# Layer 0's conditioning products in steps of four weight pieces, and two places instead of three for the split weights beside them

## The chip, the cores and the metric

The kernel runs on one core of one Trainium2 chip. The time is in device microseconds (us), from the start to the end of one execution. Engines: TensorE (PE; PEld are its weight loads), VectorE (DVE), ScalarE (ACT), GpSimd (POOL), and SyncE (SP), which here only asks for transfers (DMA).

## The reference, cut to what matters

Two layers, one of stick-breaking attention and one of gated linear attention, over 512 prompt tokens and 8 sequences of 16 sample tokens (T = 640 tokens in all, width 2048). Each layer first makes `shift, scale, gate` from a conditioning vector of each of the 9 sequences:

```python
shift, scale, gate = jnp.split(c @ w_ada[i] + b_ada[i], 3, axis=-1)   # c: 9 x 2048, w_ada[i]: 2048 x 6144
h = rmsnorm(x, norm_g[i]) * (1 + scale[:, None]) + shift[:, None]
q, k, v, zg = jnp.split(h @ w_in, 4, axis=-1)                         # layer 0: w_in 2048 x 8192
x = x + gate[:, None] * y
```

## The kernel before, in words

Big products in fp32 run as three passes on rounded halves: `halves` (L134, L135) makes of each piece a rounded part `wh` by a cast on ACT and the rest `wl` by a subtraction on DVE, and a product is `wh*hi + wh*lo + wl*hi`. A piece of weights is 128 x 1024 fp32, 512 KB.

Layer 0's input product is done mainly by `by_sevens`: the 2048 x 256 block of weights of a job (28 jobs, one for each 256 columns of q, k, v and z that earlier code leaves over) is cut in four quarters b11, b12, b21, b22, and seven products of eighths replace eight (a Strassen scheme). A job's seven products, called P1 to P7 here, are 24 matmuls each (L583, 128 x 320). Their weights are, in order: b11; b11 + t3, where t3 = b22 - b12 (L546, L550); b21; t3; b12 - b11 (L547); b21 less the second (L555); b22. The splits of these seven are called w1 to w7 here. `weights()` makes them ahead, DVE and ACT in an order that the build's scheduler sets, TensorE in the written order.

Places: raw pieces lie in four places `wb` and two `wr`. The next job's four loads are asked for by `fetch` in the course of a job; each starts when its place comes free, and the next job's b22 comes last: it takes the place that b12 leaves when w5 has been made. Split weights lie in rings: two places of `wh` and `wl` in the pool `wp`, and a third in `ring3["pool"]`, which every third call of `split` uses:

```python
third = ring3["pool"] is not None and n % 3 == 0
h, lo = ((ring3["pool"] if third else wp).tile([P, 1024], F32R, tag=t, name=t[:2], bufs=1 if third else 2)
         for t in (ring3["tags"] if third else ("wh", "wl")))
```

A split can begin when the product that last used its place has ended. With three places w(n) waits for the product three back, with two for the product two back, that is, for the start of the product just ahead.

Beside the sevens runs the side lane `rest_of_ada`: both halves of layer 0's gate, layer 1's shift and scale (four calls of `ada_mod`, L180) and a half of layer 1's gate (`ada_gate`, L222). One *step* loads `group` pieces `ar`, waits for its turn (`tiled=True`), and then multiplies each of them by the conditioning columns `cT`, 32 wide, as four 32 x 256 matmuls on four column strips of the array. `Side.tick` runs a tiled step only if `side.every` us have passed since the last by the lane's own count of TensorE's time. A step's loads are asked for as the step before frees their places.

Of the kernel before, what the change touches and what calls it, by code (L numbers as in the profile page):

```python
# [8 lines left out]
F32 = mybir.dt.float32  # L9
# [6 lines left out]
P = 128  # L16
# [25 lines left out]
def hybrid_step_kernel(ctx: ExitStack, tc: tile.TileContext, A: dict, O: list):  # L42
# [11 lines left out]
    def by(l, r):  # L54

        n = r.free_size()
        if l.dtype == F32R:
            pe["now"] += n / 2400 + 0.0133
        elif l.free_size() <= 32:
            pe["now"] += n / pe["quad"] + 0.01  # L60
        else:
            pe["now"] += n / 600 + 0.005
        return r

    def block(x):

        pe["now"] += 0.11
        return x

    def load(out, in_):  # L70
        nc.sync.dma_start(out=out, in_=in_)
# [17 lines left out]
    ad = l0.enter_context(tc.tile_pool(name="ad", bufs=1, reuse_waits="tile"))  # L89
# [9 lines left out]
    def bank(tag):  # L99
        return psum["pool"].tile([P, 512], F32, tag=tag, name=f"ps_{tag}", bufs=psum["bufs"][tag])  # L100
# [36 lines left out]
    ring3 = {"n": 0, "pool": None, "tags": ("wh", "wl")}  # L137
# [23 lines left out]
    def ada_mod(pool, ring, i, j0, ns, tag, group, pace=None, close=None):  # L161


        w, each = P * ns, 2 // ns
        src = A["w_ada"][i].rearrange("(p kt) (q m) -> p kt q m", kt=KT, q=3)
        acc = None
        for kt in range(0, KT, each * group):
            rs = []
            for k in range(kt, kt + each * group, each):
                r = ring()  # L170
                for e in range(each):
                    load(r[:, 4 * w * e:4 * w * e + 4 * w].rearrange("p (q m) -> p q m", q=2),
                         src[:, k + e, 0:2, 256 * j0:256 * j0 + 2 * w])
                rs.append(r.rearrange("p (e q c) -> p e q c", e=each, q=4))
            yield step(pace(group) if pace else 0.5, tiled=True)
            if acc is None:
                acc = bank(tag)
            for m in range(each * group):
                for q in range(4):
                    mm(acc[32 * q:32 * q + 32, :w], cT[:, kt + m, :], by(cT[:, kt + m, :], rs[m // each][:, m % each, q, :]),  # L180
                       start=kt + m == 0, stop=kt + m == KT - 1)
        if close:
            close()
        row = pool.tile([P, 256], F32, tag="ada_r", name="ada_r")[:, :w]
        dve.tensor_copy(row, acc[:, :w])
        yield step(1.5, tp=1)
        tp = bank("tp")
        for s in range(ns):
            turn_block(tp[:, P * s:P * s + P], block(row[:, P * s:P * s + P]), ident)
        v = tp[:, :P * ns].rearrange("p (s t h r) -> p t h s r", s=ns, t=2, h=2)  # L190
        for h in range(2):
            ks = slice(2 * j0 + ns * h, 2 * j0 + ns * h + ns)

            def col(c0):
                return cols[:, c0 + ks.start:c0 + ks.stop].unsqueeze(2).to_broadcast([P, ns, NSEQ])

            sh, sc, b0 = sh_t[i][:, ks, :], sc_t[i][:, ks, :], 56 + 32 * i
            dve.tensor_tensor(sh, v[:, 0, h, :, :NSEQ], col(b0), op=ALU.add)
            dve.scalar_tensor_tensor(sc, v[:, 1, h, :, :NSEQ], 1.0, col(b0 + KT), op0=ALU.add, op1=ALU.add)
            dve.tensor_tensor(sc, sc, col(16 * i), op=ALU.mult)  # L200

    def ada_gate(pool, ring, i, tag, group, cT, halves_=(0, 1)):

        src = A["w_ada"][i].rearrange("(p kt) n -> p kt n", kt=KT)
        for hf in halves_:
            bias = pool.tile([P, 256], F32, tag="ada_bg", name="ada_bg")
            acc = None
            for j in range(4):
                n0 = 2 * D + 1024 * hf + 256 * j
                load(bias[32 * j:32 * j + 32, :], A["b_ada"][i, n0:n0 + 256].partition_broadcast(32))  # L210
            for kt in range(0, KT, group):
                rs = []
                for k in range(kt, kt + group):
                    r = ring()
                    load(r, src[:, k, 2 * D + 1024 * hf:2 * D + 1024 * hf + 1024])
                    rs.append(r)
                yield step(0.5, tiled=True)
                if acc is None:
                    acc = bank(tag)
                for m, r in enumerate(rs):  # L220
                    for j in range(4):
                        mm(acc[32 * j:32 * j + 32, :256], cT[:, kt + m, :], by(cT[:, kt + m, :], r[:, 256 * j:256 * j + 256]),  # L222
                           start=kt + m == 0, stop=kt + m == KT - 1)
            dve.tensor_tensor(bias, acc[:, :256], bias, op=ALU.add)
            for j in range(4):
                store(gate_d[i][:, 1024 * hf + 256 * j:1024 * hf + 256 * j + 256], bias[32 * j:32 * j + NSEQ, :])
# [47 lines left out]
    def step(wait=0.0, tp=0, z=0, tiled=False):  # L274
        return wait, tp, z, tiled
# [68 lines left out]
    side = Side()  # L344
# [390 lines left out]
    cT = ad.tile([P, KT, 32], F32, name="cT")  # L735
    nc.gpsimd.memset(cT, 0.0)

    def ad_ring():
        return ad.tile([P, 1024], F32, tag="ar", name="ar", bufs=2)
# [3 lines left out]
    with tc.tile_pool(name="st", bufs=1, reuse_waits="tile") as st:  # L743
# [46 lines left out]
        def pace(n):  # L790
            come["n"] += n
            return max(0.0, 18.0 + 1.4 * come["n"] - pe["now"])

        def ring(tags):
            n = 0
            while True:
                tag = tags[n % len(tags)]
                yield ad_ring() if tag is None else sp.tile([P, 1024], F32, tag=tag, name="ar")
                n += 1
# [32 lines left out]
        pe["quad"] = 2400  # L832


    def rest_of_ada():
        yield step(22.0)
        yield from ada_gate(ad, ad_ring, 0, "z", 2, cT)
        for k0 in range(0, 8, 2):
            yield from ada_mod(ad, ad_ring, 1, k0, 2, "z", 2)
        yield from ada_gate(ad, ad_ring, 1, "z", 2, cT, (0,))  # L840

    with tc.tile_pool(name="wq", bufs=1, reuse_waits="tile") as wq:
        def rows0(out, p, scratch, prompt, sample):

            cs = slice(256 * p, 256 * p + 256)

            def leave(g, n, tp):
                kr = slot(12 + g % 2, (P, 2, 256), F32, "kr")
                dve.tensor_copy(kr[:, :n, :], tp)
                if scratch is not None:  # L850
                    store(scratch[256 * g:256 * g + P * n, :].rearrange("(a p) n -> p a n", p=P), kr[:, :n, :])
                if g < 2:
                    store(prompt[256 * g:256 * g + 256, cs].rearrange("(a p) n -> p a n", p=P), kr)
                else:
                    store(sample[:, cs], kr[:, 0, :])

            return as_rows(out, leave)

        def keep_key(p):
            def f(out):  # L860
                keep_in(k_d[p])(out)
                side.add(rows0(out, p, None, kp_rows, ks_rows))
            return f

        def keep_value(p):
            return lambda out: side.add(rows0(out, p, v_d[p], vp_rows, vs_rows))

        jobs = []
        for p in range(NPAIR):
            jobs += [(D + 256 * p, keep_key(p)), (256 * p, keep_in(q_d[p]))]  # L870
            if p >= 2:
                jobs.append((2 * D + 256 * p, keep_value(p)))
        jobs += [(3 * D + 256 * p, keep_in(z_d[p])) for p in range(PLAIN, NPAIR)]
        side.every = 8.0
        side.add(rest_of_ada())
        ring3["pool"] = wq
        ring3["n"] = 0
        sevens = by_sevens(h1, w_in0, wq, jobs, given)
        for _ in range(2):
            next(sevens)  # L880
        for i in range(5):
            v01 = slot(8 + i, (P, 512), F32, "v01")
            (dve.tensor_copy if i % 2 else nc.scalar.copy)(v01, acc[i])
            for p in range(2):
                move(v_d[p][P * i:P * i + P, :], v01[:, 256 * p:256 * p + 256])
            move(vp_rows[P * i:P * i + P, 0:512] if i < 4 else vs_rows[:, 0:512], v01)
        ends.close()
        drive(sevens)
        side.finish()
        h1.again(0, wq)  # L890
        ring3["pool"] = None
# [308 lines left out]
    with tc.tile_pool(name="o0", bufs=1, reuse_waits="tile") as po, ExitStack() as only_d:  # L1200
# [136 lines left out]
        wq = only_d.enter_context(tc.tile_pool(name="wq1", bufs=1, reuse_waits="tile"))  # L1337
# [90 lines left out]
        n = 0  # L1428
# [469 lines left out]
    with tc.tile_pool(name="o1", bufs=1, reuse_waits="tile") as po:  # L1898
# [3 lines left out]
        for kt in range(10, 16):  # L1902
            r = po.tile([P, T], F32, tag="rows", name="og_in", bufs=6)
            load(r, og_d[kt // 4][:, kt % 4, :])
            n = 20 + 2 * kt % 12
# [44 lines left out]
        for c in range(3):  # L1950
            drive(hs_gemm512(og1, w_out1, 512 * c, lambda a, pt: add(a, c, pt), lambda: fetch_x1(c), piece=piece,
                             k0=8, nk=8))
# [41 lines left out]
```

## Time and profile before

| | |
|---|---|
| time, median of 3 runs | 2571.93 us (2571.87 to 2578.37) |
| profiled execution | 2568.07 us, its span 2566.3 us, mean granted clock 0.979 |
| busy in the span | PE 2442.6 us (95%), PEld 84%, DVE 63%, ACT 40%, POOL 6% |
| the sevens of layer 0 | about 153.6 to 937.8 us of the span |
| steps of `rest_of_ada` | 56, from 184.6 to 739 us |

A row of the timeline gives start, duration, engine, line, operation, out<-in, shape, how many of the same were merged, and in brackets the engine's idle time before it and what ended it. Matmuls overlap: the time that one costs is the distance between starts, not its duration. A row of windows gives a stretch, its length, the busy time of each engine with its instructions, the granted TensorE clock (1.00 is 2.4 GHz, 0.50 is 1.2 GHz), the busy share of the 16 DMA engines, and GB/s. Waits are engine, line, what was waited for: us in total, times, longest.

### The profile page before, as it was taken

How to read it: one execution, taken by the hardware profiler on the slowest of the kernel's cores; microseconds unless marked ns; L12 is line 12 of the kernel's file. 1: busy time of each engine (PE TensorE's matmuls, PEld its weight loads, DVE VectorE, ACT ScalarE, POOL GpSimd, SP SyncE). 2: the span in 40 equal slices, each digit the busy share in tenths (PEclk: the TensorE clock that was granted, in tenths of full speed). 3: DMA queues.
4: the chain of work that ended last, by engine and by line, in shares of the span. 5: the costliest groups of instructions: out<-in, count | busy, mean ns of one | idle time of the engine just before them, and what ended most of it. 6: DMA issues, size and time to landing. Idle time of an engine off the chain costs nothing.

```text
span 2566.3 us, 43469 instructions
## 1 busy us (share of the span) xinstructions
PE 2442.6 (95%) x17321; PEld 2146.9 (84%) x17321; DVE 1612.7 (63%) x2493; ACT 1018.4 (40%) x1796; POOL 165.0 (6%) x385
## 2 busy tenths in 40 slices
PE   6899999999999999999999989999999998889998
PEld 5589999998999998787777767999999997766776
DVE  5565555555666656666776677666666655656566
ACT  4332222222223335565444344333333364655133
POOL 0010000000000000000000000000000014334200
PEclk8899999999999999999999999999999999999999
DMA  9966666766654366766665863344444377777464
GB/s 347 317 192 217 226 207 198 242 217 197 219 186 123 118 210 212 232 214 212 224 215 175 241 203 122 99 113 129 121 127 120 112 223 254 243 237 233 170 233 146
DMA packets 452796, 502.04 MB, mean 196 GB/s; under 512 B 26090, under 2 KB 349810, under 8 KB 452466
## 3 DMA queue, kind: packets, MB, share of 16 engines
q1 hardware_dynamic: 430210, 436.86, 53.5%
q0 software_dynamic: 16048, 51.92, 6.0%
q10 hardware_dynamic: 6336, 10.49, 1.1%
q8 instruction: 136, 2.23, 0.4%
q14 instruction: 66, 0.54, 0.1%
HBM read 410.05 MB, written 89.13 MB: 195 GB/s over the span
## 4 chain that ended last, share of the span: by engine, by line
PE 76%; DVE 8%; DMA 7%; issue 4%; ACT 3%; POOL 1%; SPq 0%; ACTq 0%; POOLq 0%; DVEq 0%
PE ps_mm L583 40%; PE ps_mm L687 10%; PE ps_mm L641 4%; PE ps_mm L507 3%; PE ps_mm L367 3%; DMA gv<-kr 2%; PE ps_tp L1061 2%; PE ps_z L180 2%; PE ps_tp L1029 1%; PE ps_z L1005 1%; DVE wl L135 1%; PE ps_tp L1106 1%; PE ps_mm L1965 1%; PE ps_z L1074 1%; ACT wh L134 1%
## 5 line engine op out<-in xcount | busy, mean ns | idle before, releaser
L583 PE MATMUL ps_mm<-sums,wh 128*128 128x320 f32 x2880 | 646.0, 312 | 5.7 <-ACT wh L134 5.7
L583 PEld LDWEIGHTS ps_mm<-sums,wh 128*128 128x128 f32 x2880 | 483.3, 189 | 14.9 <-ACT wh L134 7.1
L583 PE MATMUL ps_mm<-h,wh 128*128 128x320 f32 x2160 | 483.2, 312 | 3.8 <-DVE u L589 3.8
L583 PE MATMUL ps_mm<-sums,wl 128*128 128x320 f32 x1440 | 447.6, 311 | 1.1 <-DVE wl L135 1.1
L583 PEld LDWEIGHTS ps_mm<-h,wh 128*128 128x128 f32 x2160 | 359.1, 188 | 20.0 <-issue 14.9
L135 DVE TENSOR_TENSOR wl<-wr,wh 128x1024 fp32r<-128x1024 f32 x190 | 232.3, 1224 | 215.7 <-ACT wh L134 214.3
L134 ACT CAST wh<-wb 128x1024 fp32r<-128x1024 f32 x178 | 186.8, 1049 | 444.7 <-PE ps_mm L583 379.0
L583 PE MATMUL ps_mm<-h,wl 128*128 128x320 f32 x1080 | 333.8, 309 | 0.2 <-DVE wl L135 0.2
L134 ACT CAST wh<-wr 128x1024 fp32r<-128x1024 f32 x190 | 199.4, 1050 | 320.0 <-PE ps_mm L583 196.2
L583 PEld LDWEIGHTS ps_mm<-sums,wl 128*128 128x128 f32 x1440 | 272.4, 189 | 1.8 <-DVE wl L135 1.8
L135 DVE TENSOR_TENSOR wl<-wb,wh 128x1024 fp32r<-128x1024 f32 x178 | 217.6, 1222 | 64.1 <-ACT wh L134 63.8
L687 PE MATMUL ps_mm<-wh,ogh 128*128 128x512 f32 x460 | 201.4, 438 | 14.2 <-ACT ogh L134 10.3
L641 PE MATMUL ps_mm<-h,wh 128*128 128x320 f32 x896 | 207.2, 318 | 7.9 <-ACT wh L134 5.2
L583 PEld LDWEIGHTS ps_mm<-h,wl 128*128 128x128 f32 x1080 | 202.8, 188 | 0.5 <-DVE wl L135 0.5
L687 PE MATMUL ps_mm<-wh,ogl 128*128 128x512 f32 x460 | 182.5, 397 | 0.4 <-DVE ogl L135 0.4
L687 PE MATMUL ps_mm<-wl,ogh 128*128 128x512 f32 x460 | 181.8, 395 | 0.0
L641 PEld LDWEIGHTS ps_mm<-h,wh 128*128 128x128 f32 x896 | 150.6, 190 | 19.3 <-issue 7.0
L641 PE MATMUL ps_mm<-h,wl 128*128 128x320 f32 x448 | 139.6, 312 | 1.4 <-DVE wl L135 1.4
L687 PEld LDWEIGHTS ps_mm<-wh,ogh 128*128 128x128 f32 x460 | 87.7, 191 | 44.6 <-issue 16.8
L943 DVE TENSOR_TENSOR_SCAN k<-k,zero_c 128x544 f32<-128x544 f32 (+4 forms) x96 | 93.2, 975 | 29.5 <-ACT k L939 16.6
L687 PEld LDWEIGHTS ps_mm<-wh,ogl 128*128 128x128 f32 x460 | 87.1, 189 | 21.7 <-DVE ogl L135 1.8
L687 PEld LDWEIGHTS ps_mm<-wl,ogh 128*128 128x128 f32 x460 | 87.9, 191 | 10.6
(352 smaller groups left out, 3785.2 us busy)
## 6 DMA issues: line engine op xcount, KB each, us to landing
ar<-in_w_ada_dram SPq DMA_DIRECT2D x160, 512.0 KB
wb<-in_sb_w_in_dram SPq DMA_DIRECT2D x82, 512.0 KB
kc<-in_cache_sb_k_dram SPq DMA_DIRECT2D x64, 512.0 KB
vc<-in_cache_sb_v_dram SPq DMA_DIRECT2D x64, 512.0 KB
wb<-in_gla_w_in_dram SPq DMA_DIRECT2D x51, 512.0 KB
wr<-in_gla_w_in_dram SPq DMA_DIRECT2D x45, 512.0 KB
wr<-in_sb_w_in_dram SPq DMA_DIRECT2D x44, 512.0 KB
ar<-in_w_ada_dram SPq DMA_DIRECT2D x64, 256.0 KB
```

The costliest lines, as they stand in the source:

```text
L134: nc.scalar.copy(hi, x)
L135: (e or dve).tensor_tensor(lo, x, hi.bitcast(F32), op=ALU.subtract)
L180: mm(acc[32 * q:32 * q + 32, :w], cT[:, kt + m, :], by(cT[:, kt + m, :], rs[m // each][:, m % each, q, :]), start=kt + m == 0, stop=kt + m ...
L367: mm(acc[a], l[:, c], by(l[:, c], r[:, k2, :]), start=kt == k0 and first, stop=kt == k0 + nk - 1 and last)
L507: mm(acc[a], l, by(l, r[:, e, :]), start=j == 0 and e == 0 and begun, stop=j == 7 and e == 1 and last)
L583: mm(acc, l[:, k, :], by(l[:, k, :], r), start=start and k == 0 and first, stop=k == 7 and last, skip_group_check=True)
L641: mm(acc[nt], l[:, k, :], by(l[:, k, :], r), start=k0 == 8 and k == 0 and first, stop=k0 == 0 and k == 7 and last)
L687: mm(acc, l, by(l, r[:, e, :]), start=i == 0 and e == 0 and first, stop=i == 1 and e == 1 and last)
L943: dve.tensor_tensor_scan(kr, kr, zeros[:, :w], 1.0, ALU.mult, ALU.add)
L1005: mm(z[:, :n], q[:, hh, qs], by(q[:, hh, qs], k[:, hh, :n]), start=True, stop=True)
L1029: mm(o[:, :P], l, by(l, aT[:, kb, :]), start=kb == 0, stop=kb == qb)
L1061: turn_block(tp[:, P * c:P * c + P], block(kc[:, c, P * hh:P * hh + P]), ident)
```

## The change

A step of the conditioning products takes four pieces instead of two (`group` 4), and a turn comes every 18 us of the lane's count instead of 8. The four `ar` places are the two of the pool `ad` and two in `wq`. The third place for split weights in `wq` goes, so that this stage splits into two places (later stages keep their third). Nothing of the arithmetic changes.

```diff
-    def rest_of_ada():
-        yield step(22.0)
-        yield from ada_gate(ad, ad_ring, 0, "z", 2, cT)
-        for k0 in range(0, 8, 2):
-            yield from ada_mod(ad, ad_ring, 1, k0, 2, "z", 2)
-        yield from ada_gate(ad, ad_ring, 1, "z", 2, cT, (0,))
...
-        side.every = 8.0
+        turn = [0]
+
+        def four():
+
+            turn[0] += 1
+            return ad_ring() if turn[0] % 4 < 2 else wq.tile([P, 1024], F32, tag="ar", name="ar", bufs=2)
+
+        def rest_of_ada():
+            yield step(22.0)
+            yield from ada_gate(ad, four, 0, "z", 4, cT)
+            for k0 in range(0, 8, 2):
+                yield from ada_mod(ad, four, 1, k0, 2, "z", 4)
+            yield from ada_gate(ad, four, 1, "z", 4, cT, (0,))
+
+        side.every = 18.0
         side.add(rest_of_ada())
-        ring3["pool"] = wq
-        ring3["n"] = 0
```

On TensorE the 56 steps of 8 matmuls become 28 of 16. Counted from job 0, they stand after half of P3 in jobs 5, 8, 11, 14, 17 and 20 and after P3 in job 2; after half of P5 in jobs 1, 4, 7, 10, 13, 16 and 19; the other 14 after P1 or P6 or in P7. Layer 0's later stages and layer 1 keep TensorE's order.

DVE in job 8, from the split w5 to w7. `wl_4003` and `wl_3983` are w5, the next split is w6, then t3 of the next job out of its b22 and b12, `u` is P4's sum and `out` P5's. Before:

```order
L135 TENSOR_TENSOR wl_4003<-wb_3621,wh_4002 128x1024
L135 TENSOR_TENSOR wl_4032<-wr_3625,wh_4031 128x1024
L546 TENSOR_TENSOR t3_4106<-wb_3909,wb_3907 128x1024
L589 TENSOR_TENSOR u_3898<-ps_mm_3946,m1_3897 128x320
L547 TENSOR_TENSOR wb_3907<-wb_3907,wb_3905 128x1024
L135 TENSOR_TENSOR wl_4062<-wb_3623,wh_4061 128x1024
```

Of the change:

```order
L135 TENSOR_TENSOR wl_3983<-wb_3625,wh_3982 128x1024
L589 TENSOR_TENSOR u_3890<-ps_mm_3938,m1_3889 128x320
L135 TENSOR_TENSOR wl_4036<-wr_3629,wh_4035 128x1024
L546 TENSOR_TENSOR t3_4098<-wb_3901,wb_3899 128x1024
L589 TENSOR_TENSOR out_3888<-ps_mm_4064,u_3890 128x320
L135 TENSOR_TENSOR wl_4066<-wb_3627,wh_4065 128x1024
L547 TENSOR_TENSOR wb_3899<-wb_3899,wb_3897 128x1024
```

The splits stand one product later: w6 now follows P4's sum, and t3 stands between w6 and w7, with P5's sum where P4's was. In the seven jobs with a step in or after P3, w7 follows t3 with only a sum near it (L547 behind w7); in the others L547 stands between t3 and w7.

SP at the same place of job 8; `wb_3907` and `wb_3899` are the next job's b12, the `wr` its b21, `wb_3909` and `wb_3901` its b22. Before:

```order
L71 DMA wb_3907<-in_sb_w_in_dram 128x8x128
L74 DMA out_2_dram<-kr_3943 128x2x256
L71 DMA wr_3911<-in_sb_w_in_dram 128x8x128
L74 DMA out_2_dram<-kr_3968 128x2x256
L71 DMA ar_3998<-in_w_ada_dram 128x2x512
L74 DMA out_4_dram<-kr_3987 128x256
L71 DMA ar_4000<-in_w_ada_dram 128x2x512
L71 DMA wb_3909<-in_sb_w_in_dram 128x8x128
```

Of the change:

```order
L71 DMA wb_3899<-in_sb_w_in_dram 128x8x128
L74 DMA out_2_dram<-kr_3960 128x2x256
L74 DMA out_4_dram<-kr_3979 128x256
L71 DMA wr_3903<-in_sb_w_in_dram 128x8x128
L71 DMA ar_4014<-in_w_ada_dram 128x2x512
L71 DMA ar_4016<-in_w_ada_dram 128x2x512
L71 DMA ar_4018<-in_w_ada_dram 128x2x512
L71 DMA ar_4020<-in_w_ada_dram 128x2x512
L71 DMA wb_3901<-in_sb_w_in_dram 128x8x128
```

Four pieces of the conditioning weights instead of two now stand between b21 and b22.

DVE at the start of the stage: `wr_1677` is b11 and then P2's weight, `wl_1729` is w2, `wl_1733` w3, `v01` a copy of an earlier product. Before:

```order
L883 COPY v01_1711<-ps_mm_499 128x512
L135 TENSOR_TENSOR wl_1733<-wb_1687,wh_1732 128x1024
L550 TENSOR_TENSOR wr_1677<-t3_1693,wr_1677 128x1024
L555 TENSOR_TENSOR wb_1687<-wb_1687,wr_1677 128x1024
L135 TENSOR_TENSOR wl_1729<-wr_1677,wh_1728 128x1024
```

Of the change:

```order
L888 COPY v01_1711<-ps_mm_499 128x512
L550 TENSOR_TENSOR wr_1677<-t3_1693,wr_1677 128x1024
L135 TENSOR_TENSOR wl_1729<-wr_1677,wh_1728 128x1024
L135 TENSOR_TENSOR wl_1733<-wb_1687,wh_1732 128x1024
L555 TENSOR_TENSOR wb_1687<-wb_1687,wr_1677 128x1024
```

The sum for P2 and w2 moved ahead of w3 and of L555.

## Rows read from the trace of the kernel before

**Rows 1.** The page: busy time of TensorE (part 1) and its granted clock in 40 slices of the span (part 2).

```profile
PE 2442.6 (95%) x17321; PEld 2146.9 (84%) x17321; DVE 1612.7 (63%) x2493; ACT 1018.4 (40%) x1796; POOL 165.0 (6%) x385
PEclk8899999999999999999999999999999999999999
```

**Rows 2.** Windows: the sevens while the steps run, and after the last step.

```profile
185.00:744.00 559.00, 556.86 (x4270) 513.28 (x4263) 325.52 (x378) 154.31 (x174) 0.00 (x0) 1.00 0.67 214
744.00:938.00 194.00, 193.32 (x1320) 192.80 (x1318) 120.85 (x130) 62.57 (x74) 1.36 (x9) 1.00 0.41 124
```

**Rows 3.** Waits from 150 to 938 us.

```profile
ACT wh L134 <- PE ps_mm L583: 522.5, 185, 6.4
DVE t L546 <- DMA wb<-in_sb_w_in_dram: 41.3, 26, 3.5
PE ps_mm L583 <- ACT wh L134: 3.4, 1, 3.4
```

**Rows 4.** Timeline of TensorE around one step of two pieces (one fp32 matmul is two instructions, so 8 show as 16).

```profile
315.02 0.46 PE L583 MATMUL ps_mm<-sums,wh 128*128 128x320 f32 x2
315.46 0.46 PE L583 MATMUL ps_mm<-sums,wh 128*128 128x320 f32 x2
315.76 0.31 PE L583 MATMUL ps_mm<-sums,wl 128*128 128x320 f32 x1
316.00 1.07 PE L222 MATMUL ps_z<-ar,cT 128*32 128x256 f32 x16
317.00 0.56 PE L583 MATMUL ps_mm<-sums,wh 128*128 128x320 f32 x2
317.39 0.31 PE L583 MATMUL ps_mm<-sums,wl 128*128 128x320 f32 x1
```

**Rows 5.** Timeline of TensorE around a step of four pieces of the same shape, in an earlier stage whose own matmuls are 128x512.

```profile
96.71 0.39 PE L507 MATMUL ps_mm<-wl,h 128*128 128x512 f32 x1
96.93 0.39 PE L507 MATMUL ps_mm<-wh,h 128*128 128x512 f32 x1
97.25 1.93 PE L180 MATMUL ps_tp<-ar,cT 128*32 128x256 f32 x32
99.12 0.50 PE L507 MATMUL ps_mm<-wh,h 128*128 128x512 f32 x1
99.45 0.40 PE L507 MATMUL ps_mm<-wl,h 128*128 128x512 f32 x1
```

**Rows 6.** The instructions that read `cT` between 150 and 745 us: count, duration in ns (min/median/max), first and last start.

```profile
L180 PE MATMUL ps_z<-ar,cT x512: 379/379/403, 346.0 to 659.5; 128*32 128x256 f32 x171
L222 PE MATMUL ps_z<-ar,cT x384: 379/379/403, 184.6 to 739.0; 128*32 128x256 f32 x192
```

**Rows 7.** Timeline of all engines at the end of one product (the row at 383.43 is the next product's first): the split that was waiting for its place.

```profile
383.43 0.46 PE L583 MATMUL ps_mm<-sums,wh 128*128 128x320 f32 x2
383.64 1.05 ACT L134 CAST wh<-wb 128x1024 fp32r<-128x1024 f32 x1 [2.63 <-PE ps_mm L583]
383.73 0.31 PE L583 MATMUL ps_mm<-sums,wl 128*128 128x320 f32 x1
384.73 1.23 DVE L135 TENSOR_TENSOR wl<-wb,wh 128x1024 fp32r<-128x1024 f32 x1 [0.60 <-ACT wh L134]
```

**Rows 8.** Timelines of SP and of DVE: three loads of the next job's b22 (`wb`), what SP asked for ahead of them, and the t3 that waited for each.

```profile
398.05 0.37 SPq L71 DMA_DIRECT2D ar<-in_w_ada_dram  x1
398.47 0.54 SPq L71 DMA_DIRECT2D wb<-in_sb_w_in_dram  x1
406.48 1.23 DVE L546 TENSOR_TENSOR t<-wb 128x1024 f32<-128x1024 f32 x1 [3.08 <-DMA wb<-in_sb_w_in_dram]
407.62 0.48 DVE L589 TENSOR_TENSOR u<-ps_mm,m 128x320 f32<-128x320 f32 x1
408.02 1.22 DVE L547 TENSOR_TENSOR wb<-wb 128x1024 f32<-128x1024 f32 x1
...
512.97 1.23 DVE L135 TENSOR_TENSOR wl<-wb,wh 128x1024 fp32r<-128x1024 f32 x1 [0.37 <-ACT wh L134]
514.23 0.37 SPq L71 DMA_DIRECT2D wb<-in_sb_w_in_dram  x1
518.33 1.22 DVE L546 TENSOR_TENSOR t<-wb 128x1024 f32<-128x1024 f32 x1 [0.57 <-DMA wb<-in_sb_w_in_dram]
...
568.09 0.37 SPq L71 DMA_DIRECT2D ar<-in_w_ada_dram  x1
569.13 1.17 SPq L71 DMA_DIRECT2D ar<-in_w_ada_dram  x1
572.63 0.37 SPq L71 DMA_DIRECT2D wb<-in_sb_w_in_dram  x1
578.47 1.22 DVE L546 TENSOR_TENSOR t<-wb 128x1024 f32<-128x1024 f32 x1 [2.09 <-DMA wb<-in_sb_w_in_dram]
```

**Rows 9.** Windows: three microseconds in which two `ar` pieces move.

```profile
400.00:403.00 3.00, 3.00 (x22) 3.00 (x22) 0.83 (x1) 1.37 (x2) 0.00 (x0) 1.00 1.04 367
```

**Rows 10.** Timeline of DVE and TensorE at the start of the stage: P2 of job 0 waits for its weights.

```profile
157.77 1.21 DVE L135 TENSOR_TENSOR wl<-wb,wh 128x1024 fp32r<-128x1024 f32 x1
158.91 1.22 DVE L550 TENSOR_TENSOR wr<-t,wr 128x1024 f32<-128x1024 f32 x1
161.25 0.56 PE L583 MATMUL ps_mm<-sums,wh 128*128 128x320 f32 x2 [3.44 <-ACT wh L134]
162.57 0.63 PE L583 MATMUL ps_mm<-sums,wl 128*128 128x320 f32 x1 [0.76 <-DVE wl L135]
```

**Rows 11.** Timeline of TensorE: the transposes that end a call of `ada_mod`.

```profile
582.75 0.44 PE L189 MATMUL ps_tp<-ident,ada_r 128*128 128x128 f32 x2 [2.14 <-DVE ada_r L185]
```

**Rows 12.** Windows: after the idle time of rows 10, and after that of rows 11.

```profile
161.90:168.60 6.70, 6.03 (x22) 6.03 (x23) 4.21 (x4) 0.27 (x2) 2.07 (x4) 0.50 0.76 249
582.80:589.00 6.20, 6.20 (x43) 6.20 (x44) 4.07 (x10) 1.53 (x2) 0.00 (x0) 1.00 0.36 110
```

## The prediction

> **What bounds the kernel now.** I read the page first: TensorE is busy 95% of the span and its clock is at the upper level nearly throughout [rows 1], so a change that takes time off its path shows, and one that only moves other engines does not. Then the windows of the stage that is changed: TensorE is busy 556.86 of 559 us while the steps run and 193.32 of 194 after the last, at clock 1.00 [rows 2]. In this stage every microsecond is TensorE's, and the end can only come earlier through fewer or cheaper matmuls, a shorter start, or the last idle gaps.
>
> The waits tell what lies hidden behind that. ACT waits 522.5 us for the place of a split, 185 times, and DVE's t3 waits 41.3 us, 26 times, at most 3.5, for the landing of the next job's b22 [rows 3]. With three places neither reaches TensorE: its only long wait for a split is one of 3.4 us, at the start of the stage. So t3 is already late now, and the third place is what covers it. That is the cover which the change takes away.
>
> **Merging the steps: a gain.** Matmuls of the sevens start 0.44 us apart for three (0.147 each, so 24 make a product of 3.52). Around a step of two pieces the last own matmul starts at 315.76 and the next at 317.00 [rows 4]: 1.24, less 0.147, is 1.09. The first pair after it takes 0.39 to the next row, where two cost 0.29: 0.10 more. A step of eight costs 1.19. For sixteen the nearest rows are of an earlier stage with the same shape of step: 96.93 to 99.12 is 2.19, less 0.23 for one matmul of that stage, 1.96, and the first matmul after it takes 0.33 for 0.23, 0.10 more: 2.06 [rows 5]. Two steps of eight cost 2.39, so a pair merged saves 0.33. The trace has 896 records of these products [rows 6], two to a matmul, so 448 matmuls, 56 steps; 28 pairs save **9.3**. The bounds are nothing, if what is paid is per matmul in this stage too, and 28 x 1.19 = 33, if a sixteen cost no more than an eight; rows 5 shows that they do, so I take 9.3.
>
> **The start of the stage: a gain.** TensorE waits 3.44 us for w2 in job 0, then 0.76 for its rest [rows 10]. DVE did w3 at 157.77 ahead of the sum for P2 at 158.91 [rows 10]; in the new order that sum comes first, so the chain to w2 is earlier by one DVE operation, 1.14 (from start to start). With the L555 that also stood ahead of w2 and now doesn't, it may be 2.3, but w2's cast on ACT comes between; I take **1.2**. The idle that remains is 3.44 - 1.2, some 2.2, and behind the wait of 3.44 the clock was 0.50 for 6.7 us [rows 12], which is 3.4 us of full speed lost. I leave the fall in the sum.
>
> **The call's end: a gain.** At 582.75 TensorE idles 2.14 us for ada_r, because the copy stands on DVE behind t3 and w7 [rows 11]. In the new order that copy stands after a w3, with no wait for a load just ahead. **2.1**. Gains together: 9.3 + 1.2 + 2.1 = 12.6.
>
> **Two places: the steady splits fit.** With two places a split begins when the product two back ends. The row that shows such a start: product ends 383.43, cast at 383.64, rest at 384.73, done 385.96 [rows 7], 2.5 us after. The product that runs meanwhile takes 3.52, so 1.0 us is left over, and the rest is asked for only at the next product's third matmul, 0.29 later. Hidden, and ACT's 522.5 us of waiting grow without cost. Without that cover, that is, if DVE is held for over 1.3 us between two splits, the excess goes to TensorE. DVE's sums (0.40) and L547 (1.14) each fit singly. The one operation that can hold it longer is t3, since it waits for a load.
>
> **t3 between w6 and w7: the loss.** Let 0 be the end of P3 and of the step in or after it. w5 is done at 2.5, and its end lets SP ask for the next b22 (the row before: 512.97 + 1.23 = 514.20, asked 514.23 [rows 8]), so at 2.55. P4, P5, P6 take 3.52 each; P7 starts at 10.56 and wants w7's rest at 10.85. Behind t3 DVE has to do t3 (1.14), P5's sum (0.40) and w7's rest (1.23), with 0.05 to TensorE, 2.82 in all. t3 must start by 8.03, so at most 5.5 us after the asking. That holds for the seven jobs with a step in or after P3, where L547 stands behind w7. In the other jobs it stands ahead: 4.35, or 6.4 where a step in P5 adds 2.06.
>
> How long from asking to t3? Three rows [rows 8]: 4.10 with nothing asked shortly ahead (514.23 to 518.33), 5.84 with two `ar` pieces asked 4.5 and 3.5 ahead (572.63 to 578.47), 8.01 with the later of two asked 0.4 ahead (398.47 to 406.48). In the new order the seven jobs ask for b21 and four `ar` pieces ahead of b22; the step ends half a product, 1.76, before P3 does, and frees its places as it ends, so with the 2.55 until b22 the four are asked for some 4.5 to 3.2 us before b22, b21 some 5.0 before. Two pieces' worth of time in a window full of transfers, 367 GB/s [rows 9], makes 0.524 MB / 367 GB/s = 1.43 us a piece; the undisturbed 4.10 is then 2.67 of fixed time and 1.43 of moving. Six pieces one behind the other from b21 on, counted from b22's asking: -5.0 + 2.67 + 6 x 1.43 = 6.25. From the 5.84 instead, with two more pieces and without the small stores that moved there too (1.07 by my estimate from the 1.43): 5.84 + 2.86 - 1.07 = 7.6. I take the middle, 6.9: 1.4 us over the 5.5, in seven jobs **9.8**. For the other jobs, where 4.10 lies 0.25 under the 4.35 and a store may come between, **1.0** in all. Bounds: 4.10 gives nothing, 8.01 gives 2.5 x 7 = 17.5.
>
> A rule of the Trainium skill speaks against the change here ("DMA: Bandwidth & Descriptors", section "Queues, rings and completion order"): a DMA engine takes the descriptors of one issuer in ring order, and the count that tells of the end comes behind all earlier writes of that engine. By ring order alone the sum would be the 6.25, 0.75 a job and 5.3 in all, and the forecast 2565.6; the row at 398.47, two pieces ahead and 8.01 us, is later than such a sum (about 6), so the trace agrees on the waiting and asks more than the rule.
>
> **The rest at nothing.** The lane moves the same bytes, four pieces in some 20 us for two in some 10 (56 steps in 559 us), with DMA busy 0.67 [rows 2]. The lane ends one job earlier. Later stages keep TensorE's order; their third place only starts its count elsewhere, +-2 us.
>
> **Sum.** -12.6 + 10.8 = -1.8. The profiled execution took 2568.07, 3.86 under the median of the runs; so 2566.3 for such an execution and **2570.1** on the scale of the median, 2571.93.
>
> **Rivals.** A measurement of this kernel tells some 0.3%, 7.7 us, from no change.
>
> *A: the loads are in time.* t3 starts within 5.5 and nothing stalls. That needs 0.75 us, half a piece, less than the sum of the six: enough if SP asks for the four that much earlier against P3's end than I place them, as it does where a step frees its first places while the others are still multiplied (1.96 us for the four). For it: the 4.10 row. Against: two pieces asked just as early made 5.84 [rows 8]. Time: 2571.93 - 12.6 = 2559.3, and 2555.9 if the clock's fall at the start goes too.
>
> *C: t3 comes late enough for the clock to fall.* Place: ahead of P7's rest in the seven jobs. With b22 as late as the worst row, 8.01, TensorE idles 2.5 there: 17.5 + 1.0 - 12.6 = +5.9. An idle of 2.14 was followed by clock 1.00, one of 3.44 by 0.50 for 6.7 us [rows 10 to 12]; the point that decides lies between, and each fall costs 3.4. With two of the seven beyond it: +5.9 + 6.8 = +12.7, 2584.6; with all seven 2601. For it: the worst row has two pieces ahead, the change has four. Against: nearer pieces than those of the change.
>
> The Trainium skill has the same mechanism ("TensorE: Matmul & The Clock Gate", section "HAM oscillation — how this bites in real kernels"): waits that leave TensorE idle take the clock back to its lower level. By it C costs as worked out above; the start of the stage in this trace agrees, 0.50 after 3.44 us of idle, and the 2.14 shows that not each wait does it.
>
> *D: merging saves nothing*, a sixteen costing two eights: 2570.1 + 9.3 = 2579.4. Against: rows 5 directly, though of a stage with other matmuls.
>
> **How the numbers follow.** Main case (some stall, eaten by the merging) 0.39, A 0.33, C with falls 0.24, D 0.04. Faster by over 0.3% is A, 0.33; slower is C and half of D, which lies on the bound, 0.26; within is the rest, 0.41. The likeliest case alone reaches from 2564 to 2578 (a t3 at 6.25 or at 7.6, the later stages' 2). The range has to take in A's 2559.3 and C's 2584.6, each with the 2 of the later stages less what leaves a fifth out: 2558 to 2587.
>
> **What would show it.** Merging: steps of 32 records with some 2.2 between the own matmuls around them, 28 of them. Start: idle of about 2.2 for w2, clock 0.50 after it. Call's end: no 2.14 gap before L189. Loss: TensorE waiting for DVE's wl (L135) at the third matmul of P7 in the seven jobs, some 1.4 each, and L546's wait for b22 longer than before's 41.3 in all; none there is A, over 2.5 with clock under 1.00 behind it is C. The prediction is wrong if splits stall in every job (the 1.0 us of margin not there), or if the later stages change by more than 2.

## The result, and the profile after

The changed kernel takes 2584.99 us in the median of six runs (2580.31 to 2588.13), the kernel before 2572.64 (2571.78 to 2578.37) on the same chip; the ratio is 1.0039, with a 95% interval of 1.0028 to 1.0051. It became slower, by some 10 to 12 us. The forecast was 2570.1, no change; rival C, in the range, named 2584.6, but not the reason.

The page of the changed kernel, busy time and granted clock, against [rows 1]:

```profile
PE 2446.3 (95%) x17321; PEld 2157.4 (83%) x17321; DVE 1613.0 (62%) x2493; ACT 1017.5 (39%) x1796; POOL 164.5 (6%) x385
PEclk8899999999999999999999999999999999989999
```

The span is 2586.4 for 2566.3, TensorE's busy time 3.7 us longer: the rest is idle time. Windows of the sevens against [rows 2]:

```profile
185.00:744.00 559.00, 549.20 (x4180) 516.78 (x4180) 325.59 (x377) 154.52 (x175) 0.00 (x0) 0.99 0.63 207
744.00:940.00 196.00, 194.45 (x1362) 191.44 (x1361) 121.04 (x130) 63.03 (x74) 0.00 (x0) 1.00 0.43 131
```

TensorE now idles 9.8 us of the 559 where it idled 2.1. Waits from 150 to 948 us against [rows 3]:

```profile
ACT wh L134 <- PE ps_mm L583: 503.9, 179, 10.6
DVE t L546 <- DMA wb<-in_sb_w_in_dram: 41.1, 26, 4.4
PE ps_mm L583 <- DVE wl L135: 7.0, 11, 1.6
PE ps_mm L583 <- DVE out L589: 5.3, 6, 1.3
PE ps_mm L583 <- ACT wh L134: 2.3, 1, 2.3
```

t3 waits as long in all as before (41.1 for 41.3), but now TensorE waits behind it: 7.0 for w7's rest and 5.3 for P5's sum. The forecast had placed the whole wait at w7's rest; a part of it comes already at P7's first matmul, which needs the bank that P5's sum leaves, and that sum too stands behind t3. One step of four pieces, where [rows 4] has one of two:

```profile
378.12 0.31 PE L583 MATMUL ps_mm<-sums,wl 128*128 128x320 f32 x1
378.36 1.93 PE L180 MATMUL ps_z<-ar,cT 128*32 128x256 f32 x32
380.22 0.56 PE L583 MATMUL ps_mm<-sums,wh 128*128 128x320 f32 x2
380.62 0.31 PE L583 MATMUL ps_mm<-sums,wl 128*128 128x320 f32 x1
```

380.22 - 378.12 - 0.147 is 1.95, and 0.11 more for the first pair: 2.06, as taken from [rows 5].

A single profile misleads here: the same kernel's executions differ by up to 20 us. So this table sets three profiles of the changed kernel (one of the first result, two of the experiments) beside four of the kernel before. The sevens reach from the start of the first L583 to the end of layer 0's last (its start and the 0.147 that one takes), "behind" from there to the end of the span:

| us | before | changed |
|---|---|---|
| sevens | 784.0, 782.7, 784.7, 783.5 | 788.8, 782.8, 778.2 |
| mean | 783.7 | 783.2 |
| behind | 1628.7, 1632.6, 1639.6, 1642.6 | 1645.0, 1645.0, 1637.8 |
| mean | 1635.9 | 1642.6 |

The stage that the change touches is as long as before. What is lost, is lost behind it, where TensorE's order is that of before. The profiles show only a part of the loss: these three executions lie 5.6 us above those four in the mean, where the timed medians differ by 10 to 12.

### The profile page after: what moved, and what is told of

It is laid out like the page before. It is cut to its first block, busy times and chain, and to the rows that moved or that the text cites. A ratio compares the mean times of both kernels' runs of the same rounds, so it can differ in the third digit from the quotient of the medians.

```text
span 2586.4 us, 43478 instructions
## 1 busy us (share of the span) xinstructions
PE 2446.3 (95%) x17321; PEld 2157.4 (83%) x17321; DVE 1613.0 (62%) x2493; ACT 1017.5 (39%) x1796; POOL 164.5 (6%) x385
## 4 chain that ended last, share of the span: by engine, by line
PE 73%; DMA 11%; DVE 8%; issue 3%; ACT 3%; POOL 1%; SPq 0%; ACTq 0%; POOLq 0%; DVEq 0%
PE ps_mm L583 36%; PE ps_mm L687 10%; PE ps_mm L641 5%; PE ps_mm L367 3%; PE ps_mm L507 3%; DMA gv<-kr 2%; DMA ar<-in_w_ada_dram 2%; PE ps_tp L1066 2%; DMA wb<-in_sb_w_in_dram 2%; DVE wl L135 2%; PE ps_z L180 1%; PE ps_tp L1034 1%; PE ps_tp L1521 1%; PE ps_z L1010 1%; ACT wh L134 1%
## 5 line engine op out<-in xcount | busy, mean ns | idle before, releaser
L583 PE MATMUL ps_mm<-sums,wh 128*128 128x320 f32 x2880 | 646.3, 313 | 9.9 <-DVE out L589 5.3
L583 PEld LDWEIGHTS ps_mm<-sums,wh 128*128 128x128 f32 x2880 | 481.9, 189 | 21.1 <-issue 11.7
L583 PE MATMUL ps_mm<-h,wh 128*128 128x320 f32 x2160 | 481.3, 311 | 7.3 <-DVE u L589 7.3
L583 PE MATMUL ps_mm<-sums,wl 128*128 128x320 f32 x1440 | 448.1, 311 | 7.4 <-DVE wl L135 7.4
L583 PEld LDWEIGHTS ps_mm<-h,wh 128*128 128x128 f32 x2160 | 361.1, 188 | 11.4 <-issue 7.4
L583 PE MATMUL ps_mm<-h,wl 128*128 128x320 f32 x1080 | 334.4, 310 | 0.2 <-DVE wl L135 0.2
L583 PEld LDWEIGHTS ps_mm<-sums,wl 128*128 128x128 f32 x1440 | 272.1, 189 | 10.3 <-DVE wl L135 10.3
L687 PE MATMUL ps_mm<-wh,ogh 128*128 128x512 f32 x450 | 198.9, 442 | 12.6 <-ACT ogh L134 9.5
L583 PEld LDWEIGHTS ps_mm<-h,wl 128*128 128x128 f32 x1080 | 203.3, 188 | 0.5 <-DVE wl L135 0.5
L134 ACT CAST wh<-t 128x1024 fp32r<-128x1024 f32 x45 | 47.2, 1050 | 126.0 <-PE ps_mm L583 123.8
```

The costliest lines, as they stand in the source:

```text
L134: nc.scalar.copy(hi, x)
L583: mm(acc, l[:, k, :], by(l[:, k, :], r), start=start and k == 0 and first, stop=k == 7 and last, skip_group_check=True)
L687: mm(acc, l, by(l, r[:, e, :]), start=i == 0 and e == 0 and first, stop=i == 1 and e == 1 and last)
```

## The experiments: the sevens

**The changed kernel again, twice.**

> The changed kernel once more, for its profile. In the first profile the sevens end 2.9 us later than before and the later stages add another 17 us in jumps (4.8 at 959, 3.1 at 1270, 3.2 at 1873, some more behind 2070), each beside a lower granted clock. Theory: the stalls of the sevens are fixed by the order of the work and come again in the same jobs (5, 8, 11, 14, 17, 20, 2 and 6) within 1 us; most jumps of the later stages are chance and at least two of the three named do not come again. Rival: the change altered the later stages too (another count of the third place), then all three come again at the same places.

> The changed kernel for a third profile: its sevens took 788.8 and 782.8. Stalls before P7 in jobs 2, 5, 6, 8, 11, 14, 17 and 20 again, 13 to 20 us in all, and the rest 1640 or more if the loss behind the sevens is its own, 1629 to 1640 if it is chance.

2581.91 and 2568.13 us in these executions. From the starts of the products (a product alone 3.52, with a step 5.48), stalls at P6 and P7: 19.1 us in the first profile, 13.7 and 8.9 in these; in the seven jobs with a step in or after P3 13.0, 8.9 and 7.4, in job 6 6.1, 4.5 and 1.0. The jobs are the same but for one in the third (job 11), the sizes differ by more than the 1 us that I expected. The jumps behind the sevens came again at or near the same places in the second profile, the one near 1270 at half its size: the rival's side of that expectation.

The longest stall of the seven jobs is job 8's, 3.7 us. First profile, SP, DVE and TensorE:

```profile
399.90 3.34 SPq L71 DMA_DIRECT2D ar<-in_w_ada_dram  x4
403.96 1.23 DVE L135 TENSOR_TENSOR wl<-wb,wh 128x1024 fp32r<-128x1024 f32 x1 [4.57 <-ACT wh L134]
405.22 10.83 SPq L71 DMA_DIRECT2D wb<-in_sb_w_in_dram  x2
407.48 1.23 DVE L135 TENSOR_TENSOR wl<-wr,wh 128x1024 fp32r<-128x1024 f32 x1 [0.44 <-ACT wh L134]
412.90 1.23 DVE L546 TENSOR_TENSOR t<-wb 128x1024 f32<-128x1024 f32 x1 [4.19 <-DMA wb<-in_sb_w_in_dram]
414.04 0.48 DVE L589 TENSOR_TENSOR out<-ps_mm,u 128x320 f32<-128x320 f32 x1
414.67 0.53 PE L583 MATMUL ps_mm<-sums,wh 128*128 128x320 f32 x2 [1.11 <-DVE out L589]
415.71 0.41 PE L583 MATMUL ps_mm<-sums,wl 128*128 128x320 f32 x1 [0.51 <-DVE wl L135]
```

Four pieces asked for, then w5, then b22 at 405.22 (the row holds two loads; the first is b22). t3 starts 7.68 later, behind w6, and P7 waits first for P5's sum, then for w7's rest: the chain of the forecast. Of the 3.7 us the lateness of t3 over the 5.5 makes 2.2; the rest comes from the clock, which fell behind these two waits:

```profile
417.00:420.40 3.40, 3.40 (x14) 3.40 (x14) 2.55 (x3) 0.00 (x0) 0.00 (x0) 0.50 0.79 243
```

From asking to t3 the six jobs with half of P3 ahead of the step took 6.60 to 7.68 in this profile, where 6.9 was taken. Job 6 has another cause:

```profile
342.62 2.79 SPq L71 DMA_DIRECT2D ada_bg<-in_b_ada_dram  x4
345.45 8.29 SPq L71 DMA_DIRECT2D wb<-in_sb_w_in_dram  x2
349.44 1.23 DVE L546 TENSOR_TENSOR t<-wb 128x1024 f32<-128x1024 f32 x1 [4.41 <-DMA wb<-in_sb_w_in_dram]
351.21 0.53 PE L583 MATMUL ps_mm<-sums,wh 128*128 128x320 f32 x2 [1.34 <-DVE out L589]
353.38 0.63 PE L583 MATMUL ps_mm<-sums,wl 128*128 128x320 f32 x1 [1.64 <-DVE wl L135]
```

There the gate's bias (`ada_bg`) is asked for ahead of b22, at 342.62, and b22 is asked for at 345.45, though w5 was done at 341.51. TensorE waited 1.34 and then 1.64 us, and from within the second wait the clock was 0.50 for 6.8 us:

```profile
352.20:359.00 6.80, 5.62 (x38) 3.91 (x42) 3.88 (x4) 0.00 (x0) 0.00 (x0) 0.50 0.31 86
```

**t3 off DVE.** In `weights()`, from the second job on:

```diff
-                own.tensor_tensor(t3, b22, b12, op=ALU.subtract)
+                (nc.gpsimd if given is not None and i else own).tensor_tensor(t3, b22, b12, op=ALU.subtract)
```

> The change with layer 0's t3 computed by POOL instead of DVE from the second job on, so that w7's subtraction on DVE no longer stands behind an operation that waits for b22. Theory: the stalls before P7 (13 us in the seven jobs, 1.4 in job 2, 6 in job 6) go, the sevens end at about 924 instead of 942 and the time is some 15 to 19 us under the changed kernel, 2566 to 2570. Rival (two places are too few whatever stands on DVE): the stalls stay and the time is that of the changed kernel, 2585. A third: POOL's t3 is so slow that P2 of the next job waits, then stalls appear before P2.

2572.70 us (ratio to before 0.9990, 0.9981 to 1.0000). The stalls are gone, the sevens end at 923.9 and take 772.1. Some 0.2 us came up at P1 with a step (0.9 in job 3), the third case in small. Of the time 12.3 us came back, less than forecast; behind the sevens this profile took 1647.3.

**Steps kept out of P2 to P4.** `Side` gets a flag `barred`, tested in `tick` for tiled steps, and `by_sevens` sets it:

```diff
             nc.scalar.copy(m1, x)
             yield
+            side.barred = given is not None
...
             plus(u[:, 1], y, m1)
+            side.barred = False
             yield
```

> The change with steps kept out of the products P2 to P4, so that no four pieces are asked for shortly ahead of b22; the steps then mostly stand at the end of P4, one in each job, and the last in job 27. Theory: b22 lands about 4.1 us after it is asked for, nothing waits before P7, but for job 6 or wherever the loads of the gate's bias block SP; the sevens end at 922 to 926, and the time is 2564 to 2570. Rival (two places are too few by themselves): stalls as in the changed kernel in jobs without the burst too, 2585.

2567.88 us, ratio 0.9969 (0.9958 to 0.9980): faster than both kernels. No stall in any job; the windows, whole:

```profile
185.00:744.00 559.00, 559.00 (x4209) 536.39 (x4206) 346.56 (x388) 163.47 (x184) 0.00 (x0) 1.00 0.60 195
```

The sevens take 769.3, so the gains of the change are 783.7 - 769.3 = 14.4, for 12.6 forecast; t3 starts 4.0 us after b22 is asked for (392.13 to 396.12 in job 8). The stalls, 13.9 in the mean of the three profiles, ate all of it but 0.5.

**The four pieces on POOL's queue** (`move` for `load` where the ring is `four`).

> The change with the four pieces of a step asked for on POOL's queue instead of SP's. If b22 is late since it stands behind the four in SP's own ring, t3 starts 4.1 to 5 us after b22 is asked for in the seven jobs (6.6 to 7.7 in the change) and their stalls go, some 13 us: 2570 to 2574. If it is late since the 16 DMA engines are full whoever asked, t3 still starts 6.5 us or more after, the stalls stay and the time is 2583 to 2588.

2576.97 us (1.0023, 1.0005 to 1.0041): between the two. In the six jobs t3 came 6.3 us after the asking in the mean (5.4 to 7.2). In the three profiles of the change that mean is 7.2, 6.9 and 6.5, and 4.1 without steps in P2 to P4. So most of the delay stays when another queue asks, and whether SP's own order makes any of it is not shown by this one profile. The Trainium skill's rule on ring order ("DMA: Bandwidth & Descriptors", section "Queues, rings and completion order") speaks of the descriptors of one ring; by it alone the delay would go with the four pieces on another queue, and the trace has 6.3 for 4.1.

**Two places alone**, the kernel before without the line that gives this stage its third place:

```diff
-        ring3["pool"] = wq
         ring3["n"] = 0
```

> The kernel before with only two places for split weights in this stage, steps of two pieces every 8 us as they were. Theory: b22 with at most two pieces ahead makes t3 start 4 to 8 us after the asking; above 5.5 P7 waits, but steps in P4 to P6 give 1.2 of slack each, so some 2 to 8 us of stalls in all, less the 2.4 of the earlier start: 2571 to 2579. Rival (two places are too few by themselves): over 1 us in each of 28 jobs, 2600 and more.

2583.60 us, ratio 1.0037 (1.0024 to 1.0050), a miss. The sevens took 783.3 with stalls of 4.0, which the earlier start and the shorter wait for ada_r (1.02) nearly pay for. So two places lose 8 us in the timed runs, and by this profile it lies behind the sevens. That was the open question.

## The experiments: what is lost behind the sevens

**The third place again at the end** (from job 24 on), as the first splits of the next stage come earlier with it.

> The kernel before with two places up to job 23 and the third place from job 24 on, so that the end of the sevens and the first splits of the next stage go as before. Theory that two places at the end of the stage delay the next stage: the wait for kc behind the sevens is back at 2.5 us or less, no fall of the clock at its side, and the time is 3 to 5 us under that of two places throughout (2583.6), 2578 to 2581. Theory that what is lost behind the sevens is chance of the clock: the time is that of two places, 2582 to 2585.

2583.16 us (1.0035): as two places throughout, the wait for kc 3.5 with a fall at its side. Not this.

**The kernel before again**, three times.

> The kernel before once more, for its profile. Behind the sevens it had 9 falls of the clock, 51 us at the lower level, where five profiles of kernels with two places had 65 to 82; all five also have a fall 22 us behind the end of the sevens (waiting for kc) and one at about 1265, which the first profile of before does not have. If these two are chance, they appear here too and the stretch from the end of the sevens is some 1634 to 1640 us instead of 1628.7; if the change makes them, they are missing again and the stretch stays within 3 us of 1628.7.

> The same kernel as in the run beside it, for a third profile of before: a fall that is missing in all three profiles of before and there in all five of two places belongs to the change; one that is there in some of the three is chance.

> The kernel before for a fourth profile: sevens 782 to 785 in either case; the rest 1629 to 1640 if three places are better behind the sevens too, and over 1640 at times if the rest is chance.

2569.11, 2577.93 and 2580.26 us. The fall at kc is there in all three, that near 1265 in the third: neither belongs to the change. But the timed difference stays, so where does it arise?

**Three places, a turn every 9 us** (`side.every = 9.0` in the kernel before).

> The kernel before with a turn every 9 us instead of 8, three places as before: the steps of two pieces stand at other products, nothing else of the sevens changes, and behind the first instructions of the next stage every engine has the order that it has before. From the end of the sevens to the end three profiles of before took 1628.7, 1632.6 and 1639.6 us and seven profiles with two places 1641.0 to 1647.3. If two places in the sevens are what makes the later stages longer, this one takes 1629 to 1640 there and 2572 to 2577 in all. If any change of the sevens does it (before is a lucky meeting of idle times and clock), it takes 1641 to 1647, and 2581 to 2586.

2571.98 us (0.9990, 0.9979 to 1.0000), behind the sevens 1636.2. Not any change does it.

**The version without stalls, with the third place counted as before.**

> The version with steps kept out of P2 to P4, and with the count of the third place set back at the stage's start as before did it, so that the later stages use the third place for the same splits as before. If the shifted count is what costs in the later stages, they take 1629 to 1640 us instead of 1641 and the time is 2558 to 2564; if not, 1641 or more, and 2564 to 2570.

2565.34 us (0.9965, 0.9952 to 0.9978), behind the sevens 1650.0, though in the slowest of its twelve executions (2575.29). The time is that without the count set back: the count is not it.

**Two places alone, twice more.**

> Two places throughout, steps of two pieces, for a second profile. Its first had 783.3 us for the sevens and 1641.0 behind them, against 784.0, 782.7, 784.7, 783.8 and 1628.7, 1632.6, 1639.6, 1636.2 in four profiles with three places; timed it is 8 to 10 us slower. If what it loses lies behind the sevens, the sevens take 782 to 785 again and the rest 1640 or more. If it lies in the sevens and the first profile was a lucky one, the sevens take 787 to 793 here, with stalls before P7 in more jobs, and the rest some 1629 to 1640.

> The same kernel for a third profile, to the same end: sevens 782 to 785 and the rest over 1640, or sevens 787 to 793 and the rest 1629 to 1640.

2577.95 and 2584.34 us; sevens 783.5 and 784.2, the rest 1639.7 and 1646.3. The loss lies behind the sevens, though from soon after the end of the sevens the order of TensorE, DVE, ACT and SP is that of before.

The traces say in what the loss consists. Behind the sevens five profiles with three places take 1635.9 us in the mean, eleven with two (the change and its variants among them) 1643.7. TensorE idles 79.3 us there in the five and 82.8 in the eleven, and its clock is at the lower level for 61.4 and 69.8: 3.5 more idle and half of 8.4 are 7.7 of the 7.8.

The sevens of layer 1 show a part of it. At P5 of their jobs 4 and 8 TensorE idles 0.9 us at most in the five, and 1.2 to 2.3 in the eleven. Job 4 of the kernel before and of two places alone, the last rest of `kr` on DVE, which waits for a store, and P5's first matmul:

```profile
1738.69 0.43 DVE L135 TENSOR_TENSOR kr<-ps_tp,kr 128x256 fp32r<-128x256 f32 x1 [0.43 <-DMA gv<-kr]
1740.79 0.53 PE L583 MATMUL ps_mm<-h,wh 128*128 128x320 f32 x2 [0.55 <-DVE u L589]
```

```profile
1741.21 0.42 DVE L135 TENSOR_TENSOR kr<-ps_tp,kr 128x256 fp32r<-128x256 f32 x1 [2.37 <-DMA gv<-kr]
1743.31 0.53 PE L583 MATMUL ps_mm<-h,wh 128*128 128x320 f32 x2 [2.26 <-DVE u L589]
```

The same store is waited for 1.9 us longer. DMA by queue from 6.5 to 9.0 us after that job's start, before and with two places (packets, MB, share of 16 engines):

```profile
q1 hardware_dynamic: 895, 0.57, 86.8%
```

```profile
q1 hardware_dynamic: 921, 0.58, 85.9%
q8 instruction: 1, 0.02, 2.7%
```

A 16 KB packet on the queue of instructions comes 7.8 us after the job's start with two places, 10.4 before. Of the five profiles with three places four have it at 10.0 to 10.4; the fifth has it at 7.7, with 0.8 us of idle at P5 all the same, so that the packet's place does not decide alone. Such packets come every 19 us or so in layer 1's sevens, in which TensorE starts 256 instructions in the mean. And the count of TensorE's instructions ahead of that job differs: 25651 in all profiles with three places, 25673 to 25681 with two, since more of its matmuls have a wait instruction of their own. So the loading of program code may stand differently to the work. The count can be set by itself.

**Six matmuls more in the kernel before**, while TensorE waits for w2 in job 0:

```diff
             nc.scalar.copy(m1, x)
             yield
+            if given is not None and i == 0:
+                for _ in range(2):
+                    pad = bank("tp")
+                    for _ in range(6 // 2 + (6 % 2) * _):
+                        mm(pad[:, :32], ident, ident[:, :32], start=True, stop=True)
```

> The kernel before with six more small matmuls on TensorE (128x32, into a bank of their own, their result unused) while it waits for w2 in job 0; every other engine and all addresses are as before. In layer 1's sevens five profiles with three places idle 0.2 to 1.0 us at P5 of jobs 4 and 8, eleven with two places 1.2 to 2.3, in the very same instructions; the store gv<-kr in job 4 ends 1 us later there, and a 16 KB packet of program code moves 7.4 us after that job's start with two places, mostly 10.4 with three. TensorE has 22 to 30 more instructions ahead of that place with two places (25 in the kernel with two places alone), 12962 before. Theory: more instructions shift TensorE's code loading against the work, and it meets the stores. Then 24 more instructions alone give the other pattern: idle of 1.5 to 2.3 at P5 of jobs 4 and 8, the packet at about 7.5, layer 1's sevens 437 to 442 us instead of 433 to 438, the time 2577 to 2583. Rival (it is two places in itself, however): idle and packet as before, and 2572 to 2576.

**57 of them with two places alone.**

> Two places alone with 57 such small matmuls in job 0, 228 more instructions on TensorE, so that with the 25 of the two places it has about 253 more than before, one code packet's worth (16 KB at 64 bytes would be 256) and so nearly the old position. The start of the sevens gets longer by up to 8 us, which is not the question. Theory of the code loading: layer 1's P5 of jobs 4 and 8 idle 0.2 to 1.0 as with three places, and its sevens take 433 to 438 us. Rival: 1.2 to 2.3 of idle and 437 to 442.

The six matmuls: 2581.90 us, ratio 1.0033 (1.0021 to 1.0045), with 24 more instructions and sevens of 783.0. The packet comes 6.9 us after the job's start:

```profile
1744.52 0.42 DVE L135 TENSOR_TENSOR kr<-ps_tp,kr 128x256 fp32r<-128x256 f32 x1 [2.37 <-DMA gv<-kr]
1746.62 0.53 PE L583 MATMUL ps_mm<-h,wh 128*128 128x320 f32 x2 [1.37 <-DVE u L589]
```

The 57: 2591.37 us (1.0064). The sevens take 804.9, 21.6 more than with two places alone: 17.2 in P1 and P2 of job 0, where the matmuls stand (my 8 was too low), and most of the rest in longer stalls. But behind the sevens 1633.7, the level of three places, with two. The packet comes at 10.5, 253 instructions from before's:

```profile
1760.99 0.42 DVE L135 TENSOR_TENSOR kr<-ps_tp,kr 128x256 fp32r<-128x256 f32 x1 [0.55 <-DMA gv<-kr]
1763.10 0.53 PE L583 MATMUL ps_mm<-h,wh 128*128 128x320 f32 x2 [0.26 <-DVE u L589]
```

Both forecasts held, but for the 1.37 at job 4 with the six (1.5 or more was expected; job 8 has 2.12). Layer 1's sevens took 439.2 with the six and 435.2 with the 57, where three places have 433.1 to 438.3 and two 436.2 to 442.3.

**Eight matmuls in the version without stalls**, 32 instructions, 54 over before.

> The version with steps kept out of P2 to P4 and the count set back, with eight small matmuls on TensorE in the wait for w2 of job 0, 32 instructions more: some 54 more than the kernel before, where 22 to 30 and 24 more were bad for layer 1's sevens (437 to 442 us) and 253 more were as good as none (435). A third position of the code loading. If it is a matter of the position, layer 1's P5 idle may change against the version without the eight; if 54 more is a good place, 433 to 438 us there and 2556 to 2561 in all; if it is as bad, 2564 to 2568. I hold the two for about as likely.

2562.73 us, ratio 0.9965 (0.9952 to 0.9977); layer 1's sevens 433.9, a good position again, behind the sevens 1637.1. The ratio is that of the version without the eight, so that a gain from the position isn't shown in the time, where the experiments before it let expect some 6 to 8 us; its median lies 2.6 under. This speaks against the number of instructions as the whole cause.

## Why the prediction was wrong

- **Merging: right.** 2.06 for a step of four, 0.33 saved a pair, 9.3 in all.
- **Start: right in kind.** P1 and P2 of job 0 take 12.6 us in all three profiles of the change, 13.6 to 15.0 before; the clock still falls, for 3.4 us.
- **Call's end: right.** The idle before L189 is gone; it was 2.0 to 2.9 in four profiles of before. All gains 14.4 for 12.6, as the version without stalls has them.
- **Two places, t3 between w6 and w7: right, and its size.** In the seven jobs 13.0, 8.9 and 7.4, in the mean 9.8, where 9.8 was forecast; that the mean meets it to the tenth is luck, as single executions lie up to 3.2 off. "For the other jobs 1.0" was too small: 4.1 in the mean, nearly all of it job 6, where the bias loads block SP ahead of b22; that queue was not looked through for what comes once in a call.
- **The stage: near, in part by luck.** -0.5 us in the mean of the profiles, forecast -1.8: 1.8 more of gains and 3.1 more of stalls than forecast nearly cancel.
- **"The rest at nothing", later stages +-2: the step that failed.** They cost 6.7 us in the means of the profiles, about what two places alone (6.4) and six idle matmuls (8.1 in one profile) cost there, though TensorE's order there is the same. The prediction gave no reason for the 2 but this order, and an order that stays is not a time that stays: the change also added some 30 instructions to TensorE's stream. That 24 alone cost as much was shown in the kernel before; for the changed kernel itself the cause is inferred from it.
- **Rival C** named nearly the time, by another way. Its fall of the clock came once in the seven jobs of three profiles, in job 8 of the first (0.50 for 3.4 us behind waits of 1.11 and 0.51), and in job 6 in two. Its reading of two rows, that the deciding idle lies between 2.14 and 3.44 us, did not hold: the clock fell beside shorter waits. The Trainium skill's rule on waits ("TensorE: Matmul & The Clock Gate", section "HAM oscillation — how this bites in real kernels"), that waits of TensorE take the clock back, agrees with both: 0.50 beside the waits of job 8 and beside the 1.34 and 1.64 of job 6.
- **A** fell with the six askings of 6.60 to 7.68, over 5.5 each, in the first profile; **D** with the 2.06.

What isn't shown: how the number of instructions lengthens the later stages. That the loading of code does it fits the two experiments with idle matmuls, but not the fifth profile with three places, nor the time of the version with eight; by what one packet among 900 would delay a store is open too. Beside layer 1's sevens (some 4 us) the rest of the 6 to 8 lies in idle and lower clock at other places, which no run sets apart.

## What to carry to other kernels

A ring with one place fewer turns whatever stands late in an engine's order into a stall of the next engine; look for the operation that waits for a load, and for what its queue holds ahead of it once in a while, not only in each round. When a kernel's steps are moved, keep the asking for many pieces away from the one load that someone waits for: that alone made this change a gain, 0.997. And a change of 0.3% in a kernel of many instructions may come with their number alone: add a few idle instructions to the old kernel as a control before a cause is looked for in the order.

## What the runs showed of the hardware

Program code comes by DMA while the kernel runs: the queue of instructions moves 16 KB for every 256 of TensorE's instructions, every 19 us or so in layer 1's sevens. 24 more instructions of TensorE in a wait cost 0.33% (0.21 to 0.45); that the position of the code loading against the work is the reason is a reading, not shown. Idle of 2.70 us at one place (L1022, near 1270) was followed by no fall of the clock in three profiles of before, and by 3.4 us at the lower level in the kernel with the third place from job 24 on, with the same 2.70: the length of the idle alone does not decide there.
